# Two chunks at a time: smaller steps for norms and for the recurrence in a planned one-core kernel

## The chip, the core and the metric

The kernel runs on one core of one Trainium2 chip. TensorE (PE in the rows; PEld is its weight load) multiplies matrices, VectorE (DVE) and ScalarE (ACT) work on elements, GpSimd (POOL) does little here, and SyncE (SP) issues the loads. Each engine runs its own instructions in the order in which the program holds them, and waits where an operand or a buffer isn't ready. The metric is the time of one execution on the device, in microseconds; less is better.

## What is computed

Two transformer blocks over 256 tokens of width 1024, in float32. The first block is a self-attention with two kinds of heads, an attention to 256 memory rows, a gated feed-forward network with a short convolution, and a final norm. The second block has two layers over the latent tokens x and 256 context tokens ctx. Each layer modulates norms by a vector c and projects to three mixers: a neighbourhood attention, a two-way linear recurrence (RWKV-7) and a convolution. Layer 0 ends in a dense FFN for x and for ctx, layer 1 in a mixture of eight experts for x. Cut to its core:

```python
def first_block(x, mem, ...):
    u = rmsnorm(h, g_mix)
    h = h + norm(attention(u @ w_in)) @ w_out
    h = h + memory_cross_attention(rmsnorm(h, g_cross), rmsnorm(mem, g_mem))
    h = h + conv_ffn(rmsnorm(h, g_ffn))
    return rmsnorm(h, g_final)

def _rwkv7_scan(r, w, k, v, z, b):
    def step(S, inp):
        s_z = einsum('ghvk,ghk->ghv', S, z_t)
        S = S * w_t + s_z b_t^T + v_t k_t^T
        return S, einsum('ghvk,ghk->ghv', S, r_t)
    return lax.scan(step, zeros, (r, w, k, v, z, b))
```

The recurrence runs in both directions; each scans the context first and goes on into the latent tokens, and a norm per head (`_head_norm`) follows.

## The kernel before

Activations lie transposed, 8 chunks of 128 features by 256 tokens. A float32 product is made of three faster ones: each operand is split into a high and a low half (`whi`, `wlo` for weights; the pairs in `op`, `opM`, `fh` for activations), and `mm3` multiplies high by high, high by low and low by high. Weights come by 512 KB loads (`raw`), ScalarE rounds the high half (L306, L439) and VectorE subtracts for the low half (L307, L440). `products` (L467) emits 12 such matmuls a step, and every matmul has line L291.

The program is cut into stages by pools of buffers. B is the first block's attention beside the context's first projections and the modulation of layer 0. F+C0 is the first FFN (`first_ffn`, then `first_norm`) beside the context's recurrence (`rwkv(0, 1, ...)`) and mixing. A1 is the projections of the latent tokens (`latents`) beside the modulation of layer 1. C1 is the dense FFN of the context beside the latent recurrence (`rwkv(0, 0, ...)`) and mixing. A2 projects the context of layer 1 beside the dense FFN of x, C2 has the rest of that FFN beside a recurrence, C3 holds the last attention and recurrence, and M the experts.

What stands in what order is decided when the program is built. Each part is a Python generator that emits some instructions and then yields. `par` (L149) takes, of those that are ready, the one whose yielded cost over its weight is least, lets it emit up to its next yield, and so weaves the parts together. A yielded `Lat(wait, cost)` (L139) makes a generator unready until the others have spent `wait` in cost; it is a wait of the planner, which puts other instructions between, and no instruction of the chip:

```python
        cost = c.cost if isinstance(c, Lat) else c or 1.0
        e[0] += cost / e[3]
        spent += cost
        if isinstance(c, Lat):
            e[5] = spent + c
```

Work named `behind` fills in at its weight as long as a main part lives. The context's dense FFN (`dense_ffn(1, xc)`, called D1 below) is such work in F+C0, with weight 60, once the first FFN has stopped loading and the context's mixing is done; in A1 it is behind with 19, and in C1 it is a main part with 150 against 187.5. So whatever of it is emitted early is missing later. After that a scheduler moves single instructions within each engine's order.

A norm goes like this. `col_sums` puts sums of squares into a small bank (`sm<-bcst,ss`), `rsqrt` (L309 to L322) works on two columns on VectorE (`sc`), a matmul spreads the result over the partitions (`sm<-bcst,sc`), and `make_op` (L375) multiplies each of 8 chunks (L380) and splits it on ScalarE and VectorE (L382 to L386) for the next product. `norm_op` (L389) made all 8 chunks in one step, `first_norm` (L753) likewise. In the recurrence `rwkv` (L977) makes the unit keys `kk`, `rwkv_maps` (L1012) the decays and gates, and `rwkv_unit` (L1140) works a chunk of 128 features (i = 0, then 1, in each direction dr) through doubling steps of small matmuls (`c<-t,t`, `c<-t,zt`, `c<-cst,t`) each of which waits for the copy or the product of the step before (L301, L1260). `rwkv_scan` (L1043) carries the state (`S`, `Sb`) and ends in the norm per head.

Of the kernel before, what the change touches and what calls it, by code (L numbers as in the profile page):

```python
# [14 lines left out]
ALU = mybir.AluOpType  # L15
# [4 lines left out]
P = 128  # L20
T = 256
# [216 lines left out]
class K:  # L238
# [136 lines left out]
    def make_op(self, op, x, rb, A, B=None):  # L375

        nc = self.nc
        for c, (h, l) in enumerate(op):
            y = self.t("t1", [P, T])
            nc.vector.scalar_tensor_tensor(out=y, in0=x[:, c, :], scalar=A(c), in1=rb, op0=ALU.mult, op1=ALU.mult)  # L380
            if B is None:
                nc.scalar.activation(h, y, AF.Copy)  # L382
                nc.vector.tensor_tensor(out=l, in0=y, in1=h.bitcast(F32), op=ALU.subtract)
            else:
                nc.scalar.activation(h, y, AF.Identity, bias=B(c))  # L385
                nc.vector.scalar_tensor_tensor(out=l, in0=y, scalar=B(c), in1=h.bitcast(F32), op0=ALU.add,  # L386
                                               op1=ALU.subtract)

    def norm_op(self, x, A, B=None, tag="op"):  # L389
# [4 lines left out]
        self.make_op(op, x, rb, A, B)  # L394
        yield Lat(1.5)
# [303 lines left out]
    def first_attn(self, x, op):  # L699
# [35 lines left out]
        yop = self.new_op()  # L735
        for g in range(2):
            rb = yield from self.rstd(self.norm_sum(ys[g], C=4), 512, 1e-6)
            self.make_op(yop[4 * g:4 * g + 4], ys[g], rb, lambda c: self.v("g_out", 4 * g + c))
# [14 lines left out]
    def first_norm(self, x):  # L753
# [6 lines left out]
        yield 1.0  # L760
# [216 lines left out]
    def rwkv(self, l, s, u, S0, need_out, st):  # L977
# [10 lines left out]
        ps = self.head_sums(sq, "c0")  # L988
        nv = self.t("sc", [P, 16])[:, :8]
        nc.vector.tensor_scalar(out=nv, in0=ps[:, 0:8], scalar1=1.0, scalar2=1e-12, op0=ALU.mult, op1=ALU.add)  # L990
        kb = self.head_bc(self.rsqrt(nv, 8), "c0")
        kk = self.t("kk", [P, 2, T])
        for i in range(2):
            nc.vector.scalar_tensor_tensor(out=kk[:, i, :], in0=k_[:, i, :], scalar=self.v(f"k_k{l}", i),
                                           in1=kb[:, i, :], op0=ALU.mult, op1=ALU.mult)
# [8 lines left out]
        yield 2.0  # L1004
# [7 lines left out]
    def rwkv_maps(self, l, dr, u, kk, vt, need_out, st):  # L1012
# [7 lines left out]
        nc.gpsimd.memset(th[64:65, :], 1.0)  # L1020
        pp = self.ps2(tag)
# [16 lines left out]
        yield 1.7  # L1038
# [4 lines left out]
    def rwkv_scan(self, l, s, dr, u, S0, need_out, st):  # L1043
# [84 lines left out]
        rb = self.head_bc(self.rsqrt(nv, 8), tag)  # L1128
# [11 lines left out]
    def rwkv_unit(self, dr, i, sw, r, kk, kd, b, vt, tag, need_out, st):  # L1140
# [36 lines left out]
        ZB, ZK = self.t("zt", [P, 2, 2, P]), self.t("zt", [P, 2, 2, P])  # L1177
        px = self.ps2(tag).rearrange("p h (c e s) -> p h c e s", c=4, e=2)
# [476 lines left out]
    def program(self):  # L1655
# [66 lines left out]
        run(par((then(self.first_ffn(x), self.first_norm(x)), 173),  # L1722
# [126 lines left out]
```

## Time and profile before

| | us |
|---|---|
| median of 3 runs (lowest to highest) | 2905.23 (2900.95 to 2911.19) |
| the profiled execution | 2904.22 |
| its span in the trace | 2902.0 |
| PE busy | 2721.5 |
| DVE busy | 2130.2 |
| ACT busy | 1703.9 |

The profiled execution had a mean granted clock of 0.959 of 2.4 GHz. Rows of the trace name a line of the kernel, the engine, the operation and out<-in by the program's names without numbers; a bracket gives the engine's idle time just before and what ended it. `acc` is the bank of the FFNs, `accA` that of projections, `c` (c0, c1) that of the recurrence's two directions, `sm` the small one and `md` that of the modulation.

### The profile page before, as it was taken

Reading aid. Unit: us, or ns where it says so; the run is one execution under the profiler, and the core shown is the slowest. Engines: PE = TensorE matmul, PEld = TensorE weight load, DVE = VectorE, ACT = ScalarE, POOL = GpSimd, SP = SyncE. Lnnn points to the kernel's source line nnn. Section 1 sums busy time; section 2 is a strip of 40 time slices with the busy share of each in tenths; the row PEclk is TensorE's granted clock in tenths of the full one; section 3 lists DMA queues with packets and bytes.
Section 4 is the critical chain, followed back from the end, with each engine's and each line's share of the span. In section 5 each row is a group of like instructions: output and inputs, shape, how many; then the busy total and the mean of one; then the engine's idle time right before and its main releaser. Section 6 shows DMA issues by size and latency. Waiting matters only on the chain.

```text
span 2902.0 us, 55553 instructions
## 1 busy us (share of the span) xinstructions
PE 2721.5 (94%) x22026; PEld 2340.4 (81%) x22026; DVE 2130.2 (73%) x3912; ACT 1703.9 (59%) x2709; POOL 79.8 (3%) x229
## 2 busy tenths in 40 slices
PE   7899989999799899999998878799999999999998
PEld 5788888999787688999997866688888878887886
DVE  4458657777668466777566864689888889989897
ACT  4455555554454355455444553478777777777775
POOL 0000000100000000000000010000000000000000
PEclk9899998999899999999999987799999999999998
DMA  7666432345466723444443221479899999999994
GB/s 269 230 196 196 154 101 89 125 125 153 147 215 223 236 85 100 146 147 152 140 139 107 92 59 29 201 282 364 342 347 359 350 350 354 358 338 356 365 353 168
DMA packets 144022, 619.81 MB, mean 214 GB/s; under 512 B 31044, under 2 KB 38536, under 8 KB 100744
## 3 DMA queue, kind: packets, MB, share of 16 engines
q1 hardware_dynamic: 143752, 616.17, 61.0%
q8 instruction: 175, 2.87, 0.4%
q14 instruction: 95, 0.78, 0.1%
HBM read 615.04 MB, written 1.07 MB: 212 GB/s over the span
## 4 chain that ended last, share of the span: by engine, by line
PE 75%; DVE 8%; ACT 4%; issue 2%; DMA 2%; POOL 0%; SPq 0%; ACTq 0%; POOLq 0%; DVEq 0%
PE acc L291 42%; PE py L291 10%; PE accA L291 8%; PE sm L291 6%; PE c L291 6%; DVE wlo L307 1%; DVE wlo L440 1%; PE md L291 1%; PE sm L1571 1%; ACT whi L306 1%; PE accA L505 0%; DMA raw<-mod_w 0%; ACT whi L439 0%; DVE x L939 0%; DVE t L380 0%
## 5 line engine op out<-in xcount | busy, mean ns | idle before, releaser
L440 DVE TENSOR_TENSOR wlo<-raw,whi 128x1024 fp32r<-128x1024 f32 x666 | 779.4, 1220 | 79.8 <-ACT whi L439 73.0
L306 ACT ACTIVATE whi<-raw 128x512 fp32r<-128x512 f32 x764 | 474.3, 629 | 502.1 <-PE acc L291 259.7
L307 DVE TENSOR_TENSOR wlo<-raw,whi 128x512 fp32r<-128x512 f32 x764 | 521.3, 689 | 330.2 <-ACT whi L306 316.8
L439 ACT ACTIVATE whi<-raw 128x1024 fp32r<-128x1024 f32 x666 | 676.7, 1058 | 105.6 <-PE py L291 60.8
L291 PE MATMUL acc<-whi,op 128*128 128x512 f32 (+1 forms) x2048 | 620.8, 379 | 0.0
L291 PE MATMUL acc<-op,whi 128*128 128x256 f32 x2880 | 561.4, 294 | 8.7 <-ACT op L385 3.6
L291 PEld LDWEIGHTS acc<-op,whi 128*128 128x128 f32 x2880 | 460.1, 196 | 36.3 <-issue 13.8
L291 PEld LDWEIGHTS acc<-whi,op 128*128 128x128 f32 x2048 | 378.6, 189 | 71.5 <-issue 3.0
L291 PE MATMUL acc<-op,wlo 128*128 128x256 f32 x1440 | 414.7, 288 | 10.3 <-DVE wlo L307 10.3
L291 PE MATMUL acc<-wlo,op 128*128 128x512 f32 (+1 forms) x1024 | 393.0, 384 | 2.5 <-DVE wlo L440 1.4
L291 PEld LDWEIGHTS acc<-op,wlo 128*128 128x128 f32 x1440 | 281.5, 196 | 13.1 <-DVE wlo L307 12.7
L291 PE MATMUL py<-whi,ht 128*128 128x512 f32 x896 | 291.2, 396 | 0.5 <-ACT ht L306 0.5
L291 PE MATMUL accA<-opM,whi 128*128 128x256 f32 x1408 | 272.0, 292 | 7.7 <-ACT opM L306 3.5
L291 PEld LDWEIGHTS accA<-opM,whi 128*128 128x128 f32 x1408 | 225.0, 196 | 23.7 <-issue 7.7
L291 PEld LDWEIGHTS acc<-wlo,op 128*128 128x128 f32 x1024 | 193.2, 189 | 53.6 <-DVE wlo L440 17.6
L291 PE MATMUL acc<-fh,whi 128*128 128x256 f32 x1056 | 206.1, 293 | 3.0 <-ACT fh L306 1.9
L291 PE MATMUL accA<-opM,wlo 128*128 128x256 f32 x704 | 202.4, 288 | 1.5 <-DVE wlo L307 1.3
L291 PEld LDWEIGHTS py<-whi,ht 128*128 128x128 f32 x896 | 168.7, 188 | 39.3 <-ACT ht L306 0.9
L291 PE MATMUL py<-wlo,ht 128*128 128x512 f32 x448 | 180.6, 403 | 0.3
L291 PEld LDWEIGHTS acc<-fh,whi 128*128 128x128 f32 x1056 | 165.4, 192 | 18.4 <-issue 9.6
L291 PE MATMUL acc<-fh,wlo 128*128 128x256 f32 x528 | 150.4, 285 | 1.9 <-DVE wlo L307 1.9
L291 PEld LDWEIGHTS accA<-opM,wlo 128*128 128x128 f32 x704 | 137.3, 195 | 4.5 <-issue 2.2
(338 smaller groups left out, 3337.2 us busy)
## 6 DMA issues: line engine op xcount, KB each, us to landing
raw<-moe_up SPq DMA_DIRECT2D x112, 1024.0 KB, 7.0
raw<-moe_gate SPq DMA_DIRECT2D x111, 1024.0 KB, 6.8
raw<-moe_down SPq DMA_DIRECT2D x110, 1024.0 KB, 6.8
raw<-w_in SPq DMA_DIRECT2D x120, 512.0 KB, 3.7
raw<-mod_w SPq DMA_DIRECT2D x96, 512.0 KB, 4.5
raw<-ffn_gate SPq DMA_DIRECT2D x44, 512.0 KB, 3.6
raw<-ffn_up SPq DMA_DIRECT2D x44, 512.0 KB, 3.6
raw<-ffn_down SPq DMA_DIRECT2D x40, 512.0 KB, 3.7
```

Source lines behind the costliest of these rows:

```text
L291: return self.nc.tensor.matmul(out, lhsT, rhs, start=start, stop=stop, **k)
L306: self.nc.scalar.activation(hi, src, AF.Copy)
L307: self.nc.vector.tensor_tensor(out=lo, in0=src, in1=hi.bitcast(F32), op=ALU.subtract)
L439: self.nc.scalar.activation(hi, raw[:, k:k + g, :], AF.Copy)
L440: eng.tensor_tensor(out=lo, in0=raw[:, k:k + g, :], in1=hi.bitcast(F32), op=ALU.subtract)
L1571: nc.tensor.transpose(pt[:, c * P:(c + 1) * P], h[:, c * P:(c + 1) * P], self.ident)
```

## The change

Nothing is computed otherwise. `make_op` and `first_norm` now yield after every second chunk with a planner's wait of 1.4 and a cost of 0.2 (which `norm_op` and `first_attn` hand on), so that other parts' instructions stand between the pairs; the waits behind the whole norm go. In `rwkv` the transposes of v come first, and waits stand before the sums, before the spreading of the reciprocal root, and at the end. The maps, the unit and the scan's norm get declared waits. In F+C0 the weight of the first FFN falls from 173 to 155, so that the context's part beside it gets a larger share. All engines hold as many instructions as before, but for one more load of an activation table on ScalarE.

```diff
@@ make_op, norm_op, first_attn @@
                 nc.vector.scalar_tensor_tensor(out=l, in0=y, scalar=B(c), in1=h.bitcast(F32), op0=ALU.add,
                                                op1=ALU.subtract)
+            if c % 2:
+                yield Lat(1.4, 0.2)
...
         op = self.new_op(tag)
-        self.make_op(op, x, rb, A, B)
-        yield Lat(1.5)
+        yield from self.make_op(op, x, rb, A, B)
         return op
...
-            self.make_op(yop[4 * g:4 * g + 4], ys[g], rb, lambda c: self.v("g_out", 4 * g + c))
+            yield from self.make_op(yop[4 * g:4 * g + 4], ys[g], rb, lambda c: self.v("g_out", 4 * g + c))
@@ first_norm @@
             if c % 2:
                 self.add_squares(x, c // 2)
-        yield 1.0
+                yield Lat(1.4, 0.2)
@@ rwkv @@
-        ps = self.head_sums(sq, "c0")
...
-        kb = self.head_bc(self.rsqrt(nv, 8), "c0")
-        kk = self.t("kk", [P, 2, T])
...
         self.copy(vt.rearrange("p a b -> p (a b)"), pv)
-        yield 2.0
+        yield Lat(1.0, 0.6)
+        ps = self.head_sums(sq, "c0")
...
+        rn = self.rsqrt(nv, 8)
+        yield Lat(3.2, 0.3)
+        kb = self.head_bc(rn, "c0")
+        kk = self.t("kk", [P, 2, T])
...
+        yield Lat(1.0, 1.0)
@@ rwkv_maps @@
         nc.gpsimd.memset(th[64:65, :], 1.0)
+        yield Lat(0.7, 0.1)
...
         st["kd"][dr] = kd
-        yield 1.7
+        yield Lat(0.9, 1.6)
@@ rwkv_scan @@
-        rb = self.head_bc(self.rsqrt(nv, 8), tag)
+        rn = self.rsqrt(nv, 8)
+        yield Lat(3.0, 0.2)
+        rb = self.head_bc(rn, tag)
@@ rwkv_unit @@
         ZB, ZK = self.t("zt", [P, 2, 2, P]), self.t("zt", [P, 2, 2, P])
+        yield Lat(1.2, 0.2)
@@ program, F+C0 @@
-        run(par((then(self.first_ffn(x), self.first_norm(x)), 173),
+        run(par((then(self.first_ffn(x), self.first_norm(x)), 155),
```

What that does to the order is seen at three places. The first is PE at the start of A1. Before, 48 of D1's matmuls (`acc_9159<-op_9063` and its kin; op_9063 and op_9064 are the context's normed operand) stand behind `first_norm`'s spreading, and then come the modulation (`md`), the sums and the spreading of A1's norm, and its first products (`accA`):

```order
L291 MATMUL acc_9159<-op_9064,whi_9210 128x256
L291 MATMUL acc_9159<-op_9063,wlo_9211 128x256
L291 MATMUL md_9140<-raw_9141,cs_193 32x512 x2
L291 MATMUL md_9140<-raw_9142,cs_193 32x512 x2
L291 MATMUL md_9140<-raw_9226,cs_193 32x512 x2
L291 MATMUL md_9140<-raw_9227,cs_193 32x512 x2
L291 MATMUL sm_9190<-bcst_70,ss_9102 128x1 x4
L291 MATMUL sm_9234<-bcst_70,sc_9198 128x128 x2
L291 MATMUL acc_9295<-op_9063,whi_9273 128x256
L291 MATMUL acc_9295<-op_9064,whi_9273 128x256
L291 MATMUL accA_9318<-opM_9237,whi_9310 128x256
L291 MATMUL accA_9318<-opM_9238,whi_9310 128x256
```

Now 612 matmuls of D1 stand behind `first_norm`'s spreading, and more of them between the modulation, the sums (sm_10115) and the spreading (sm_10161):

```order
L291 MATMUL acc_10001<-op_9063,wlo_10017 128x256
L291 MATMUL md_10069<-raw_10070,cs_193 32x512 x2
L291 MATMUL md_10069<-raw_10071,cs_193 32x512 x2
L291 MATMUL acc_10001<-op_9063,whi_10032 128x256
...
L291 MATMUL acc_10102<-op_9063,wlo_10081 128x256
L291 MATMUL sm_10115<-bcst_70,ss_9078 128x1 x4
L291 MATMUL acc_10102<-op_9063,whi_10098 128x256
...
L291 MATMUL md_10069<-raw_10154,cs_193 32x512 x2
L291 MATMUL sm_10161<-bcst_70,sc_10123 128x128 x2
L291 MATMUL acc_10102<-op_9063,whi_10137 128x256
```

So some 560 matmuls of D1 moved from behind A1's norm to ahead of it and into it; A1 itself holds some 650 of D1 in either order.

The second place is PE in the latter half of C1, where the units i = 1 of both directions take their doubling steps (`c_...`, one name a direction and step). Before, 12 matmuls of D1 (`acc_13334`) stand between one direction's step and the other's:

```order
L291 MATMUL c_2379_13424<-t_2373_13385,zt_13025 64x64 x8
L291 MATMUL c_2379_13424<-cst_72,t_2373_13385 64x64 x8
L291 MATMUL c_2382_13445<-t_2375_13404,t_2376_13406 64x64 x8
L291 MATMUL acc_13334<-op_9063,whi_13408 128x256
L291 MATMUL acc_13334<-op_9064,whi_13408 128x256
L291 MATMUL acc_13334<-op_9063,wlo_13409 128x256
...
L291 MATMUL c_2387_13477<-t_2380_13441,t_2381_13443 64x64 x8
L291 MATMUL c_2389_13488<-t_2383_13454,zt_12975 64x64 x8
L291 MATMUL c_2389_13488<-cst_72,t_2383_13454 64x64 x8
L291 MATMUL acc_13513<-fh_13112,whi_13458 128x256
```

Now the same steps stand with nothing between:

```order
L291 MATMUL c_2523_14284<-t_2518_14259,t_2519_14261 64x64 x8
L291 MATMUL c_2525_14295<-t_2521_14280,t_2522_14282 64x64 x8
L291 MATMUL c_2527_14306<-t_2524_14293,zt_13969 64x64 x8
L291 MATMUL c_2527_14306<-cst_72,t_2524_14293 64x64 x8
L291 MATMUL c_2530_14327<-t_2526_14304,zt_14000 64x64 x8
L291 MATMUL c_2530_14327<-cst_72,t_2526_14304 64x64 x8
L291 MATMUL c_2533_14348<-t_2528_14323,t_2529_14325 64x64 x8
L291 MATMUL c_2535_14359<-t_2531_14344,t_2532_14346 64x64 x8
L291 MATMUL c_2537_14370<-t_2534_14357,zt_13969 64x64 x8
L291 MATMUL c_2537_14370<-cst_72,t_2534_14357 64x64 x8
```

D1's last matmul now stands at the start of the units i = 1. Before, 385 of D1's matmuls stood between there and the end of the norm per head, 48 among the mixing's products, and 216 behind them; of the 385 seven are left.

The third place is DVE at the start of F+C0, where the first FFN's operand (`op`, L380 and L383) and the recurrence's maps and first unit (`kd`, `d`, L1033 to L1170 before, L1038 and on now) are made. Before, the unit keys `kk` were followed by the maps and the unit:

```order
L994 SCALAR_TENSOR_TENSOR kk_4735<-u_82,vec_68,c_879_4726 128x256 x2
L1033 TENSOR_SCALAR kd_4754<-d_886_4753,vec_68,lv_148_724 128x256 x2
L1035 TENSOR_TENSOR kd_4754<-kd_4754,u_82 128x512
L1036 TENSOR_TENSOR d_886_4753<-d_886_4753,kk_4735 128x512
L1033 TENSOR_SCALAR kd_4772<-d_891_4771,vec_68,lv_148_724 128x256
L1164 TENSOR_TENSOR t_905_4819<-u_81,ptp_4806 128x4x64
...
L1170 TENSOR_TENSOR t_906_4822<-d_886_4753,t_901_4808 128x2x128
L380 SCALAR_TENSOR_TENSOR t_914_4848<-x_66,vec_68,sm_4843 128x256
...
L383 TENSOR_TENSOR op_4847<-t_914_4848,op_4846 128x256
L383 TENSOR_TENSOR op_4847<-t_915_4852,op_4846 128x256
```

Now the operand's chunks come straight after `kk`:

```order
L1006 SCALAR_TENSOR_TENSOR kk_4762<-u_82,vec_68,c_885_4753 128x256 x2
L380 SCALAR_TENSOR_TENSOR t_890_4770<-x_66,vec_68,sm_4765 128x256
L380 SCALAR_TENSOR_TENSOR t_891_4774<-x_66,vec_68,sm_4765 128x256
L380 SCALAR_TENSOR_TENSOR t_900_4801<-x_66,vec_68,sm_4765 128x256
L383 TENSOR_TENSOR op_4769<-t_890_4770,op_4768 128x256
L383 TENSOR_TENSOR op_4769<-t_891_4774,op_4768 128x256
...
L383 TENSOR_TENSOR op_4769<-t_906_4824,op_4768 128x256
L1038 TENSOR_SCALAR kd_4792<-d_898_4791,vec_68,lv_144_708 128x256
L383 TENSOR_TENSOR op_4769<-t_907_4828,op_4768 128x256
L1038 TENSOR_SCALAR kd_4792<-d_898_4791,vec_68,lv_144_708 128x256
L1040 TENSOR_TENSOR kd_4792<-kd_4792,u_82 128x512
```

The first FFN's chunks passed twelve instructions of the maps and the unit.

## Rows read from the trace of the kernel before

**Rows 1.** Page, part 1: busy time and share of each engine, instructions
```profile
PE 2721.5 (94%) x22026; PEld 2340.4 (81%) x22026; DVE 2130.2 (73%) x3912; ACT 1703.9 (59%) x2709; POOL 79.8 (3%) x229
```

**Rows 2.** Page, part 4: the chain that ended last, by engine
```profile
PE 75%; DVE 8%; ACT 4%; issue 2%; DMA 2%; POOL 0%; SPq 0%; ACTq 0%; POOLq 0%; DVEq 0%
```

**Rows 3.** Windows: stretch, length, busy (instructions) by engine, granted clock, DMA share, GB/s
```profile
758.80:778.10 19.30, 7.85 (x44) 5.67 (x45) 13.98 (x37) 8.23 (x17) 2.18 (x2) 0.67 0.42 134
765.50:779.00 13.50, 5.87 (x24) 5.28 (x25) 11.05 (x29) 5.71 (x12) 2.18 (x2) 0.50 0.32 92
424.20:454.70 30.50, 22.80 (x92) 17.55 (x93) 17.32 (x62) 14.68 (x24) 3.74 (x17) 0.50 0.11 35
278.00:298.00 20.00, 15.11 (x81) 13.45 (x80) 16.80 (x53) 7.98 (x17) 0.15 (x2) 0.74 0.48 154
85.00:104.00 19.00, 11.69 (x48) 6.41 (x47) 10.85 (x34) 8.89 (x22) 0.00 (x0) 0.64 0.77 259
1081.00:1177.00 96.00, 89.86 (x1319) 81.26 (x1316) 66.53 (x172) 46.53 (x90) 9.80 (x26) 0.97 0.32 98
1109.10:1129.20 20.10, 20.10 (x480) 18.38 (x483) 13.39 (x29) 8.75 (x18) 0.00 (x0) 1.00 0.27 82
1542.10:1558.50 16.40, 11.31 (x299) 9.51 (x290) 7.96 (x27) 7.56 (x16) 1.16 (x6) 1.00 0.01 2
1751.90:1768.90 17.00, 15.92 (x208) 10.99 (x210) 8.35 (x32) 7.02 (x21) 1.08 (x1) 0.50 0.01 2
1850.00:2880.00 1030.00, 1016.60 (x4618) 821.34 (x4618) 900.91 (x920) 775.18 (x886) 0.00 (x0) 0.99 0.90 339
```

**Rows 4.** Windows, PE's instructions on tile acc alone, in C1's second half
```profile
1081.00:1177.00 96.00, 55.12 (x385) 48.24 (x385) 5.56 (x11) 1.75 (x3) 0.97 0.32 98
```

**Rows 5.** Timeline of PE, A1's start: start, length, instruction, [idle before <-releaser]
```profile
763.48 1.05 PE L291 MATMUL sm<-bcst,ss 128*128 128x1 f32 x8 [2.85 <-DVE ss L333]
...
766.96 1.22 PE L291 MATMUL sm<-bcst,sc 128*128 128x128 f32 x4 [2.42 <-DVE sc L321]
...
771.14 0.79 PE L291 MATMUL accA<-opM,whi 128*128 128x256 f32 x2 [2.53 <-ACT whi L306]
...
775.58 0.58 PE L291 MATMUL acc<-op,wlo 128*128 128x256 f32 x1 [3.65 <-DVE wlo L307]
```

**Rows 6.** Timeline of PE, C0's start
```profile
448.29 1.23 PE L291 MATMUL c<-cst,d 128*128 128x128 f32 x4 [1.75 <-ACT d L1032]
...
450.87 2.08 PE L291 MATMUL c<-t,t 64*128 64x128 f32 x16 [1.35 <-DVE t L1170]
...
452.88 0.79 PE L291 MATMUL acc<-op,whi 128*128 128x256 f32 x2
```

**Rows 7.** Timeline of PE, doubling steps in the tails of C2 and C3
```profile
1542.17 0.41 PE L291 MATMUL c<-t,t 64*64 64x64 f32 x16
...
1546.21 0.46 PE L291 MATMUL c<-t,t 64*64 64x64 f32 x16 [0.19 <-ACT t L301]
...
1747.97 0.46 PE L291 MATMUL c<-t,t 64*64 64x64 f32 x16
...
1750.83 0.46 PE L291 MATMUL c<-t,t 64*64 64x64 f32 x16 [2.39 <-ACT t L301]
```

**Rows 8.** Timeline of PE, six single waits
```profile
91.17 2.37 PE L291 MATMUL md<-raw,cs 128*32 128x512 f32 x6 [3.61 <-DMA raw<-mod_w]
...
331.52 0.38 PE L291 MATMUL acc<-op,wlo 128*128 128x256 f32 x1 [3.49 <-DVE wlo L307]
...
1032.37 1.16 PE L291 MATMUL c<-t,t 64*128 64x128 f32 x16 [1.87 <-DVE t L1170]
...
1563.77 1.22 PE L291 MATMUL sm<-bcst,sc 128*128 128x128 f32 x4 [4.34 <-DVE sc L321]
...
1621.89 1.45 PE L291 MATMUL c<-t,t 64*128 64x128 f32 x12 [2.50 <-DVE t L1170]
...
1813.40 0.91 PE L291 MATMUL sm<-bcst,sc 128*64 128x128 f32 x6 [3.58 <-DVE sc L321]
```

More of the change, by code (lines that the diff above doesn't have):

```diff
@@ L987, in rwkv @@
             nc.scalar.activation(sq[:, i, :], k_[:, i, :], AF.Square, scale=self.v(f"k_k{l}", i))
-        ps = self.head_sums(sq, "c0")
-        nv = self.t("sc", [P, 16])[:, :8]
-        nc.vector.tensor_scalar(out=nv, in0=ps[:, 0:8], scalar1=1.0, scalar2=1e-12, op0=ALU.mult, op1=ALU.add)
-        kb = self.head_bc(self.rsqrt(nv, 8), "c0")
-        kk = self.t("kk", [P, 2, T])
-        for i in range(2):
-            nc.vector.scalar_tensor_tensor(out=kk[:, i, :], in0=k_[:, i, :], scalar=self.v(f"k_k{l}", i),
-                                           in1=kb[:, i, :], op0=ALU.mult, op1=ALU.mult)
         vt = self.t("vt", [P, 2, T])
@@ L1003, in rwkv @@
         self.copy(vt.rearrange("p a b -> p (a b)"), pv)
-        yield 2.0
+        yield Lat(1.0, 0.6)
+        ps = self.head_sums(sq, "c0")
+        nv = self.t("sc", [P, 16])[:, :8]
+        nc.vector.tensor_scalar(out=nv, in0=ps[:, 0:8], scalar1=1.0, scalar2=1e-12, op0=ALU.mult, op1=ALU.add)
+        rn = self.rsqrt(nv, 8)
+        yield Lat(3.2, 0.3)
+        kb = self.head_bc(rn, "c0")
+        kk = self.t("kk", [P, 2, T])
+        for i in range(2):
+            nc.vector.scalar_tensor_tensor(out=kk[:, i, :], in0=k_[:, i, :], scalar=self.v(f"k_k{l}", i),
+                                           in1=kb[:, i, :], op0=ALU.mult, op1=ALU.mult)
+        yield Lat(1.0, 1.0)
         yield from par(*[(self.rwkv_maps(l, dr, u, kk, vt, need_out, st), 45) for dr in range(2)],
```

## The prediction

> **What bounds the kernel now.** The first view is the busy time by engine: TensorE works 2721.5 us of a span of 2902.0, 94% [rows 1], and three quarters of the chain that ended last are its matmuls [rows 2]. The change removes no matmul, so at most the 180 us in which TensorE stands still, and what its lower clock costs, can be won. The second view is the table of stretches [rows 3]. In the last 1030 us, the experts, TensorE is busy 1016.6 us at a granted clock of 0.99: nothing to win, and the change doesn't touch that stage. What can be won lies before 1850 us, in a handful of places where a norm or the start of a recurrence leaves TensorE without work, and each is paid twice: by the idle time, and by the clock, which stands at 0.50 (1.2 instead of 2.4 GHz) in and after most of them. The third view, the order of time on TensorE, says who ends those waits: mostly the short norm operations on VectorE, or the low half of a weight (L307) that stands behind norm chunks on VectorE [rows 5, 6, 8].
>
> The sum below is made against the profiled execution, 2904.2 us, which is 1.0 us under the median of 2905.2.
>
> **Part 1, the start of A1 (a gain).** From 758.8 to 778.1 us TensorE has 7.85 us of work in 19.3 us [rows 3]. Four waits, 2.85, 2.42, 2.53 and 3.65 us, make 11.45 us [rows 5]; from 765.5 to 779.0 the clock is at 0.50, and 5.87 us of matmuls ran there that would take half, 2.9 us less [rows 3]. That is 14.4 us in all. The new order puts 564 more of D1's matmuls ahead of A1's norm and some between its steps. They need only the context's operand, which is there, and weights whose loads are queued. So the norm's steps on VectorE run under them. What can remain: D1's own splits share VectorE with the norm's chunks, as the wait of 3.65 us for L307 shows. I take 12, between 9 and 14. The wait of the final norm of block one just before stays; no free work can pass it in the new order.
>
> **Part 2, the start of F+C0 (a gain).** From 424.2 to 454.7 us TensorE is busy 22.8 of 30.5 us, all of it at 0.50 [rows 3]. The first FFN begins only at 452.88 us [rows 6], since its operand stands behind twelve operations of the recurrence's maps and unit on VectorE. Now it comes ahead of them, some 12 us earlier. Then the waits of 1.75 and 1.35 us [rows 6] are filled, 3.1 us, and the clock can rise earlier: at full speed the last 12 us would lose up to half. What is queued behind the chunks is the recurrence, which runs beside the FFN and ends before it. I take 6.5, with 3 (the waits alone) and 12 as ends.
>
> **Part 3, norms of the first block (a gain).** From 278 to 298 us 4.9 us are idle and the clock is 0.74, which costs 5 us more [rows 3]; the cross attention's norm leaves a wait of 3.49 us for a low half behind chunks [rows 8]. Pairs of chunks let the split in between. Of the 13 us I take 7.5, for both places together, since other streams' steps are short there; the ends are 0 and 13.
>
> **Part 4, the recurrences elsewhere (a gain).** The declared waits aim at waits such as 1.87 us at the start of C1, 2.50 us in C3 and 3.58 us at its last norm per head [rows 8]. They make 7.95 us, and there are smaller ones like them. In C3 there is attention to put between. I take 10 with the clock's part, from 0 to 15. Gains so far: 12 + 6.5 + 7.5 + 10 = 36 us.
>
> **Part 5, C1's latter half loses its cover (a loss).** What D1 fills at A1's start it doesn't fill in C1. Its matmuls cost the same wherever they stand, so this is no loss by itself; the loss is what they covered. From 1081 to 1177 us TensorE is busy 89.86 of 96 us [rows 3], 55.12 us of it by 385 of D1's matmuls, 0.143 us each [rows 4]. Without 378 of them 54.1 us leave, and 35.8 us of the recurrence's own work remain. How long does that take bare? The doubling steps from 1109.1 to 1129.2 us, four pairs, are all busy with 96 of D1's between [rows 3]: 20.1 less 13.7 leaves 6.4 us of own work. A bare pair took 4.04 us in C2's tail (1542.17 to 1546.21) and 2.86 us in C3's (1747.97 to 1750.83) [rows 7], so four take 11.4 to 16.2 us, and TensorE is busy 56% or 40%. The whole bare tail of C2 is busy 11.31 of 16.4 us, 69% [rows 3]. At 69% the 35.8 us take 52, at 56% 64. The half of C1 had 6.1 us idle already; so the exposed time is 52 - 35.8 - 6.1 = 10, or 22. With a lower clock it is more: from 1751.9 to 1768.9, at 0.50, 15.92 us of matmuls ran that would take about 8 at full speed [rows 3], and the upper end is some 34. I take 22, nearest the paired steps, which are the bulk of the half.
>
> Here a rule speaks against the change. The rows show both levels in bare recurrences: 1.00 in C2's tail with 69% busy, 0.50 in C3 [rows 3]. The Trainium skill, page "TensorE: Matmul & The Clock Gate", section "HAM oscillation — how this bites in real kernels", says that waits between bursts of matmuls let the array fall back to its lower rate, so that each burst starts slow. C3's stretch agrees with it, C2's tail doesn't; by the rule the loss would be the 34, and that is the second rival.
>
> **Part 6, smaller losses.** A2's norms were covered by D1's rest and now stand behind the mixing bare: the like wait at the end of C2 is 4.34 us [rows 8], and some of one is there already, so 2.5 (0 to 5). In the attention of the first block the modulation's matmuls go ahead of the projections, four more loads of 512 KB, and TensorE waits for such a load 3.61 us already [rows 8]; 2 MB at 259 GB/s [rows 3] are 8 us, partly beside softmax work, so 4 (0 to 8). The memory attention's first head has fewer projections beside it: 2 (0 to 4). The further load of a table on ScalarE costs nothing, hidden by an engine that is busy 59% [rows 1]; uncovered it would add a microsecond or two. Losses: 22 + 2.5 + 4 + 2 = 30.5 us.
>
> **The sum.** 2904.2 - 36 + 30.5 = 2898.7, and against the median 2899.7: I forecast **2900 us**, 0.2% less. A measurement of this kernel tells no change from one of about 0.3%, 8.7 us, so this is no change. Its own range is 2890 to 2912.
>
> **Rivals.** (a) Faster: the bare recurrence is cheap. If all of C1's half goes at the 69% of C2's tail and full clock, the loss there is 10 instead of 22, and with the smaller losses near 2 instead of 8.5 the time is 2899.7 - 12 - 6.5 = 2881. A half measure gives 2890. For it: C2's tail, at full clock throughout. Against it: the paired steps, 40 to 56%.
>
> (b) Slower: the bare half of C1 runs at the lower clock. The loss there is then 34 instead of 22, and A2's bare norms start slow too, 5 instead of 2.5; if the norms of the first block give nothing besides (0 instead of 7.5), the time is 2899.7 + 12 + 2.5 + 7.5 = 2922, and without that last 2914. It decides once the half takes longer than about 70 us bare, where it had 96 with 54 of D1's in it. For it: C3's stretch at 0.50. Against it: C2's tail.
>
> (c) The fills are worthless: the norms' waits move instead of vanishing, because VectorE has to make the same chunks and D1's low halves beside them. Then A1's start gives 9, C0's 3, the others nothing, 12 in all against the same 30.5: 2923 us. Against it: VectorE is idle 5 of the 19.3 us at A1's start [rows 3], and D1 gives it one split in 12 matmuls. That the planner's waits change nothing is excluded by the order itself, at A1 and C1.
>
> **How the numbers follow.** The forecast has 0.40, (a) 0.36, (b) 0.15, (c) 0.09. A fifth left out at the far ends of (a) and of (b) and (c) gives 2879 to 2921. Faster by over 0.3% is (a), 0.36, and a little of the forecast's lower end, 0.02: 0.38. Slower is (b) and (c), less what of them stays within 0.3%: 0.22. The rest, 0.40, is no change.
>
> **What would show it.** After the change the start of A1 should hold no wait over 1 us on TensorE between the final norm of block one and the first projection but the spreading's own, and a clock near 1.00; the first FFN should begin some 12 us sooner after the unit keys. C1's latter half should be about 64 us long, from the first product of the units i = 1 to the end of the norm per head, and idle for about 28 of them, with its clock telling (a) from (b). A half under 55 us would make me wrong towards faster, one over 75 us towards slower. The experts should take the same 1030 us. If the waits at A1's start are still there, with VectorE as their releaser, it is (c).

## The result: slower by 0.6%

The changed kernel took 2923.57 us, median of 12 runs (2915.34 to 2929.61), beside 2903.93 us of the kernel before (12 runs, 2895.37 to 2911.50). The ratio is 1.0063, with a 95% interval of 1.0050 to 1.0076. I had forecast 2900 us, no change, in a range of 2879 to 2921. The measured time lies above that range, and the kernel became slower, which I had held to be less likely than faster.

The page of the changed kernel answers [rows 1] and [rows 2]: the span went from 2902.0 to 2920.6 us, and TensorE is busy for 22.6 us more with the same number of instructions. The page alone doesn't say which of them took longer. The chain could be followed over a third of the span only, so its shares aren't compared.

```profile
PE 2744.1 (94%) x22026; PEld 2354.5 (81%) x22026; DVE 2130.8 (73%) x3912; ACT 1702.7 (58%) x2710; POOL 80.9 (3%) x229
...
PE 34%; DVE 2%; ACT 1%; issue 1%; DVEq 0%; ACTq 0%
```

The stretches that the prediction named look as follows in the changed kernel (stretch, length, busy time and instructions of PE, PEld, DVE, ACT and POOL, granted clock, DMA share, GB/s). They answer [rows 3].

```profile
430.60:461.30 30.70, 26.52 (x103) 22.07 (x104) 19.08 (x65) 15.17 (x26) 4.03 (x17) 0.50 0.11 35
444.00:461.30 17.30, 16.84 (x57) 13.16 (x56) 10.08 (x24) 10.97 (x19) 4.03 (x17) 0.50 0.00 1
764.80:838.00 73.20, 70.54 (x564) 69.53 (x564) 51.00 (x87) 36.98 (x60) 4.25 (x3) 0.97 0.55 169
838.00:872.00 34.00, 33.46 (x257) 27.84 (x256) 21.72 (x49) 15.47 (x30) 0.00 (x0) 1.00 0.75 255
1158.00:1225.00 67.00, 53.07 (x982) 44.03 (x982) 43.38 (x135) 25.38 (x57) 7.26 (x22) 0.83 0.07 21
1850.00:2900.00 1050.00, 1031.04 (x4747) 835.40 (x4747) 912.10 (x945) 785.80 (x904) 0.00 (x0) 0.99 0.90 336
```

The reader is to see three things. The run of D1 (764.8 to 838) and A1's norm behind it (838 to 872) are dense at nearly full clock, so the waits of [rows 5] are gone. C1's latter half (1158 to 1225) is bare: 67 us, 13.9 of them idle, at a clock of 0.83. And the start of F+C0 (430.6 to 461.3) is denser than before, 26.5 of 30.7 us against 22.8 of 30.5, but is still wholly at 0.50.

To see where the 18.6 us of the two profiled executions come from, I cut both at the same events on TensorE: the first matmul of F+C0's recurrence, the sums of block one's final norm, the first matmul of C1's recurrence, the first product of C1's mixing, and the first matmul of C2's and of C3's recurrence. The rows count the FFNs' matmuls (tile acc) in each stretch, first in the kernel before and then in the changed kernel:

```profile
427.10:745.20 318.10, 213.17 (x1584) 196.63 (x1584) 45.16 (x79) 12.21 (x22) 0.96 0.40 125
745.20:1003.00 257.80, 92.00 (x624) 82.16 (x624) 10.13 (x20) 2.98 (x5) 0.95 0.66 210
1003.00:1176.50 173.50, 98.20 (x696) 86.97 (x696) 10.45 (x21) 2.95 (x5) 0.98 0.32 99
1176.50:1316.30 139.80, 57.23 (x416) 55.27 (x416) 9.07 (x19) 1.71 (x3) 0.96 0.50 157
```

```profile
433.30:754.80 321.50, 219.67 (x1584) 201.58 (x1584) 45.17 (x79) 12.23 (x22) 0.95 0.39 124
754.80:1083.40 328.60, 172.49 (x1272) 160.63 (x1272) 20.54 (x41) 5.30 (x9) 0.98 0.65 208
1083.40:1224.80 141.40, 45.88 (x314) 39.88 (x312) 8.52 (x18) 1.18 (x2) 0.91 0.21 64
1224.80:1334.70 109.90, 21.17 (x152) 19.85 (x152) 0.68 (x1) 1.18 (x2) 0.95 0.46 147
```

In each fence the rows are F+C0, A1 from the final norm on, C1 up to the mixing, and mixing with A2. The last three hold 1736 of these matmuls in either kernel, but 624, 696 and 416 became 1272, 312 and 152 (two of the row's 314 began before the stretch). So these three stretches are compared as one: 571.1 us before, 579.9 after, 8.8 us lost. F+C0 lost 3.4 us, the program up to F+C0 6.2 us, and all behind C2's start 0.2 us (18.6 less the others).

### The profile page after: what moved, and what is told of

The parts are those of the page before. It is cut to its first block, busy times and chain, and to the rows that moved or that the text cites. A ratio compares the mean times of both kernels' runs of the same rounds, so it can differ in the third digit from the quotient of the medians.

```text
span 2920.6 us, 55563 instructions
## 1 busy us (share of the span) xinstructions
PE 2744.1 (94%) x22026; PEld 2354.5 (81%) x22026; DVE 2130.8 (73%) x3912; ACT 1702.7 (58%) x2710; POOL 80.9 (3%) x229
## 5 line engine op out<-in xcount | busy, mean ns | idle before, releaser
L291 PEld LDWEIGHTS accA<-opM,whi 128*128 128x128 f32 x1408 | 225.8, 196 | 24.1 <-issue 6.9
```

The costliest lines, as they stand in the source:

```text
L291: return self.nc.tensor.matmul(out, lhsT, rhs, start=start, stop=stop, **k)
```

## The experiments

Every kernel ran in 5 rounds beside the kernel before on the same chip; ratios are to those runs, with 95% intervals. The lengths of stretches come from one profiled execution of each kernel, cut as above; such an execution lay up to 12 us from its kernel's median, so only differences that come back in several kernels are used.

### Each edit alone

The first four kernels are the kernel before with one group of edits each. The diffs are the hunks of the change: `first_norm` for e1, `make_op`, `norm_op` and `first_attn` for e2, `rwkv`, `rwkv_maps`, `rwkv_scan` and `rwkv_unit` for e3, and the number 155 for e4.

> The kernel before, with the one edit that the final norm of block one yields after each pair of chunks. In the order of TensorE D1's matmuls move ahead of A1's norm, and 620 small matmuls of C1's latter half stand bare (before: 164). Theory 1, lost cover: A1's start gains 6 us, C1's half loses 13, the time is 2904 + 7 = 2911. Rival, the bare half costs nothing and the loss is elsewhere: 2904 - 6 = 2898.

> The kernel before, with the one edit that the operands of norms are made two chunks at a time. Theory 1: the modulation goes ahead of the attention of block one (12 of its rows before the first products there, before: 8) and costs 5 us by waiting for loads, the norms of block one give back about as much as they lose: 2909. Rival: the pairs win the idle time of those norms, as predicted: 2904 + 4 - 7.5 = 2900.

> The kernel before, with the declared waits of the recurrence alone. Theory 1: the start of C0 gives nothing, since the clock stays at its lower level until as late as before, and C2 and C3 lose some 6 us: 2908. Rival, as predicted: the waits win 6.5 us at C0's start and 10 in the others: 2888.

> The kernel before, with the weight of the first FFN 155 instead of 173 and nothing else. Theory 1: the context's part ends somewhat earlier beside the FFN and nothing is uncovered: within 3 us of 2904. Rival: the larger share is what lets D1 start early and uncovers C1: 2910 or more.

| edit alone | median us | ratio | interval |
|---|---|---|---|
| e1, final norm in pairs | 2911.54 | 1.0008 | 0.9997 to 1.0019 |
| e2, operands in pairs | 2911.96 | 1.0012 | 0.9998 to 1.0026 |
| e3, recurrence's waits | 2888.20 | 0.9922 | 0.9905 to 0.9939 |
| e4, share 155 | 2910.56 | 1.0021 | 1.0004 to 1.0038 |

The recurrence's waits are a clear gain of 0.8%, as the prediction had it and against my theory after the result. The share alone is a small loss. The other two alone can't be told from no change, though e1's trace shows both sides of the exchange (its one profile was 10 us above its median): D1 had 1284 matmuls between the final norm and C1 instead of 624. The four logs of the ratios sum to -0.0037, 11 us faster; together the edits were 18 us slower. So the edits don't add up, and the question became which of them interact ("meet" in what follows).

### Each edit left out

Four kernels are the changed kernel with one group as before.

> The changed kernel, with the final norm of block one in one step as before. The four edits alone sum to some 11 us less than before, all together cost 18 more, so 29 us come from two of them meeting. Theory 2: it is the pairs of the final norm with the recurrence's waits. They leave C1's latter half bare (here 142 small matmuls stand bare, with all edits 662), and declared waits there have nothing to put between: 2895. Rivals, another pair: 2921.

> The changed kernel, with the operands of norms made in one step as before. Theory 2: the pair is not in it, so only what the operands cost alone goes, 3 us: 2920. Theory 3, the operand's pairs ahead of the maps at C0's start are what takes the recurrence's gain away: 2892.

> The changed kernel, without the declared waits of the recurrence. All theories of a meeting with the recurrence's waits: the other three edits sum to 12 us alone, so 2916. If the three meet with each other instead: 2925 or more, with 620 small matmuls bare in C1's half.

> The changed kernel, with the weight of the first FFN 173 as before. Theory 2: only the 6 us of the share alone go: 2917; 524 small matmuls stand bare in C1's half instead of 662, which may win a few us more. Theory 4, the share meets the recurrence's waits, so that the context's part runs ahead of its cover in F+C0: 2890.

| left out | median us | ratio | interval |
|---|---|---|---|
| u1, final norm's pairs | 2905.36 | 0.9988 | 0.9967 to 1.0009 |
| u2, operands' pairs | 2903.52 | 0.9988 | 0.9971 to 1.0005 |
| u3, recurrence's waits | 2921.09 | 1.0062 | 1.0038 to 1.0087 |
| u4, share 155 | 2904.59 | 0.9992 | 0.9979 to 1.0005 |

No single pair is to blame: three of the four groups, left out, give some 20 us back each. The theory of one meeting pair fell. And in the company of the others the recurrence's waits are worth nothing (u3 against all four), though alone they win 0.8%. u2 shows more: its D1 has 1320 matmuls between the final norm and C1 and only 264 in C1, more uneven than the changed kernel, and yet the 20 us are back.

### What carries the recurrence's gain, and what the cover is worth

x3 is the kernel before with one wait alone; x1 is the changed kernel with the weight of D1 behind A1 lowered, which keeps D1 for C1; x4 is the kernel before with the recurrence's waits and the final norm's pairs, and x2 is x4 with the same lower weight.

```diff
@@ x3: rwkv_scan, before @@
-        rb = self.head_bc(self.rsqrt(nv, 8), tag)
+        rn = self.rsqrt(nv, 8)
+        yield Lat(3.0, 0.2)
+        rb = self.head_bc(rn, tag)
@@ x1 and x2: program, A1 @@
-                behind=(ffn, 19)))
+                behind=(ffn, 4)))
```

> The changed kernel, with the context's FFN behind A1 at weight 4 instead of 19. So less of it is emitted in A1, and C1's latter half is covered again (176 small matmuls stand bare, with the change 662). Lost cover as a cause: C1 gets back some 13 us and A1 gives up some 5: 2915. Rival, the bare half isn't what costs: 2923 or more, as A1 loses fill.

> The kernel before, with the recurrence's waits, the final norm of block one in pairs, and the context's FFN behind A1 at weight 4, which keeps C1 covered (142 bare). If both gains add up where the cover is kept: 2888 for the waits, 10 less at A1's start: 2878. If A1 needs the fill that is taken from it: 2888 or more.

> The kernel before, with one declared wait alone, that before the spreading in the scan's norm per head (3.0). Theory: this one carries the recurrence's gain, since it lets the norms of both directions run beside each other: 5 us at C1's end, 9 after C3, 3 in F+C0: 2888 to 2890. Rival, the gain is spread over the maps, the unit and the keys: 2900.

> The kernel before, with the recurrence's waits and the final norm of block one in pairs, weight 19 in A1 as before, so that C1's half is bare (692). Compared with the run at weight 4 it shows what the cover is worth. Lost cover: 10 us won in A1 and 16 lost in C1 against the recurrence's waits alone, 2894. Rival, a bare half is worse under declared waits: 2904.

| kernel | median us | ratio | interval |
|---|---|---|---|
| x1, changed, D1 at 4 in A1 | 2922.00 | 1.0057 | 1.0038 to 1.0075 |
| x2, waits, final norm's pairs, D1 at 4 | 2890.39 | 0.9945 | 0.9927 to 0.9963 |
| x3, the scan's wait alone | 2893.72 | 0.9945 | 0.9926 to 0.9963 |
| x4, waits, final norm's pairs | 2898.37 | 0.9975 | 0.9955 to 0.9994 |

x3 shows that one wait has 0.55% of the 0.78%. The order of time on TensorE at C1's norm per head, of the kernel before and then of x3, shows one place where it acts. Before, the two directions' reciprocal roots ran one behind the other, and the second one's spreading waited 3.62 us on VectorE. With the wait the planner emits both sums first, the chains run beside each other, D1 fills, and both spreadings follow without any idle time, in 1.97 us for 32 matmuls:

```profile
1168.94 1.09 PE L291 MATMUL sm<-bcst,sc 128*64 128x128 f32 x16 [0.58 <-DVE sc L321]
...
1174.64 1.97 PE L291 MATMUL sm<-bcst,sc 128*64 128x128 f32 x16 [3.62 <-DVE sc L321]
```

```profile
1165.50 1.97 PE L291 MATMUL sm<-bcst,sc 128*64 128x128 f32 x32
```

This place is 2 to 3 us of the 16 (C1 took 171.1 us in x3 and 173.5 before). The stages behind C2's start were 5.1 us shorter and F+C0 2.7; the rest isn't located.

x1 shows that giving C1 its cover back by starving A1 wins nothing that can be measured. Its rows on tile acc (A1, C1, mixing with A2) don't say why: C1 has its 696 matmuls again and A1 has 768, most of them in the run ahead of its norm, but A1, C1 and A2 together take 569.3 us, 10.6 less than in the changed kernel. This execution lay 12 us under its median, so a gain that its stretches show and its median lacks is left open. I had expected 2915, if the bare C1 were what costs; so that isn't shown by this run.

```profile
752.10:1032.00 279.90, 105.81 (x768) 97.55 (x768) 11.15 (x22) 3.51 (x6) 0.97 0.65 203
1032.00:1197.60 165.60, 98.92 (x696) 87.14 (x696) 13.56 (x28) 2.37 (x4) 1.00 0.33 104
1197.60:1321.40 123.80, 37.42 (x272) 35.84 (x272) 4.86 (x10) 1.75 (x3) 0.96 0.50 155
```

x4 against e3 has the final norm's pairs, and with them the run of D1, beside the recurrence's waits: 0.9975 against 0.9922, the intervals apart. There the run costs 0.5%, though alone (e1) it cost nothing that can be told. At the lower weight (x2) 0.3% of it seem to come back, but the intervals of x2 and x4 touch.

### The share, and pairs in one place

y1 is the kernel before with the recurrence's waits (e3) and pairs in A1's norm alone; y2 is e3 with the first FFN's weight at 200; y3 has both; y4 is the changed kernel at 200. (The flag in the cut goes through to `make_op` and turns its yields on.)

```diff
@@ y1 and y3: project @@
-        op = yield from self.mod_op(x, l, 0, s, "opM")
+        op = yield from self.mod_op(x, l, 0, s, "opM", l == 0 and s == 0)
@@ y4: program, F+C0 @@
-        run(par((then(self.first_ffn(x), self.first_norm(x)), 155),
+        run(par((then(self.first_ffn(x), self.first_norm(x)), 200),
```

> The kernel before, with the recurrence's waits and with pairs of chunks in A1's norm alone. If pairs pay where other work stands ready (the context's FFN and the modulation): A1 loses 75 us instead of 86 and the time is 2888 - 8 = 2880. If pairs cost wherever they stand: 2890 or more.

> The kernel before, with the recurrence's waits and the weight of the first FFN 200 instead of 173. If the share costs by its size (155 cost some 6 to 8 us in F+C0): 5 us less there, 2883. If 173 lies at the best or any change costs: 2888 or more.

> The kernel before, with the recurrence's waits, pairs in A1's norm alone and the weight 200. If both gains hold and add up: 2876. Else the better of the two others.

> The changed kernel, with the weight of the first FFN 200 instead of 155. C1's latter half is covered in this order (142 small matmuls bare instead of 662), since the context's mixing ends later and D1 starts later. If the share is what the four together fail by, since it both thins F+C0 and lets D1 run early: 2900 or less. If the meeting is between the other edits: 2915 or more.

| kernel | median us | ratio | interval |
|---|---|---|---|
| y1, waits, pairs in A1's norm | 2889.08 | 0.9938 | 0.9915 to 0.9960 |
| y2, waits, share 200 | 2887.85 | 0.9930 | 0.9907 to 0.9953 |
| y3, waits, both | 2880.40 | 0.9916 | 0.9889 to 0.9944 |
| y4, changed, share 200 | 2884.79 | 0.9923 | 0.9900 to 0.9946 |

y4 is the largest single step of all: one number, 155 to 200, takes some 40 us from the changed kernel. In this order the context's mixing ends only at 737.8 us, behind the sums of the final norm (734.9 us); the context's own norm, which D1 needs, comes after that, and the run of D1 ahead of A1's norm is gone. The rows on tile acc (F+C0, A1, C1, mixing with A2) have 624, 708 and 406 matmuls again. A1, C1 and A2 take 561.1 us together instead of 579.9, and F+C0 306.4 instead of 321.5:

```profile
428.50:734.90 306.40, 217.23 (x1584) 199.82 (x1584) 45.17 (x79) 12.27 (x22) 0.95 0.38 127
734.90:987.00 252.10, 88.42 (x624) 79.61 (x624) 10.06 (x20) 2.97 (x5) 0.98 0.69 218
987.00:1156.40 169.40, 100.85 (x708) 89.42 (x708) 10.45 (x21) 2.96 (x6) 0.99 0.31 102
1156.40:1296.00 139.60, 55.05 (x406) 52.92 (x404) 9.03 (x19) 1.75 (x3) 0.96 0.48 159
```

On top of the recurrence's waits neither the pairs in A1 (y1) nor the share (y2) wins anything that can be told, so both of those expected gains failed, although the profiles show them in their stages: A1 took 254.7 us in y1 and 263.8 in e3, and F+C0 302.1 in y2 and 311.5 in e3. y3 has the lowest median, but its interval and those of e3, y1, y2 and y4 overlap widely: the versions at 2880 to 2889 us can't be ranked by these runs.

### The run of D1 by itself

The last two kernels separate the share from the run of D1. The context's FFN may form its operand as in the changed kernel, but emit products only when the final norm is written; z1 keeps 155, z2 has 173.

```diff
@@ dense_ffn @@
         op = yield from self.mod_op(x, 0, 1, s, "op")
+        if s:
+            yield lambda: self.normed
@@ first_norm @@
                 yield Lat(1.4, 0.2)
+        self.normed = True
```

> The changed kernel at its share of 155, but the context's FFN may begin its products only when the final norm of block one is written. So its run of 612 matmuls ahead of A1's norm is gone (48 as before), C1's latter half is covered (142 small matmuls bare) and all else is as changed. If the run is the cause: 2923 less the 20 us of C1 and with a few back at A1's start, 2905, like the change without the final norm's pairs. If the share costs in F+C0 alone: 2918 or more.

> The same at the share of 173. If the share costs a further 8 us in F+C0: 2897, between the gated one at 155 and the 2885 at 200. If the run is all: the same as the gated one at 155.

| kernel | median us | ratio | interval |
|---|---|---|---|
| z1, changed, D1 held back | 2901.77 | 0.9993 | 0.9977 to 1.0009 |
| z2, the same at 173 | 2896.64 | 0.9972 | 0.9960 to 0.9984 |

z1 gives back 20 us (1.0063 to 0.9993, intervals far apart) by nothing but the gate that holds D1 back. Its rows (F+C0, A1, C1, mixing with A2) stand against those of the changed kernel above: the last three take 561.7 us instead of 579.9, 18 less, and F+C0 is as long as there.

```profile
428.80:752.20 323.40, 219.96 (x1584) 201.70 (x1584) 45.20 (x79) 12.22 (x22) 0.95 0.38 123
752.20:1001.70 249.50, 93.07 (x624) 81.87 (x624) 10.16 (x20) 2.95 (x5) 0.98 0.67 216
1001.70:1174.30 172.60, 102.63 (x720) 90.89 (x720) 10.44 (x21) 2.96 (x6) 0.98 0.31 99
1174.30:1313.90 139.60, 53.93 (x394) 51.85 (x392) 9.07 (x19) 1.74 (x3) 0.96 0.48 160
```

With all of TensorE's instructions counted, A1 and C1 of the changed kernel and then of z1 show where the 18 us are:

```profile
754.80:1083.40 328.60, 312.56 (x2348) 266.21 (x2349) 211.61 (x492) 159.16 (x313) 11.46 (x15) 0.98 0.65 208
1083.40:1224.80 141.40, 123.51 (x2047) 106.96 (x2045) 94.94 (x260) 66.22 (x130) 15.74 (x45) 0.91 0.21 64
```

```profile
752.20:1001.70 249.50, 233.25 (x1700) 186.56 (x1701) 159.30 (x406) 116.68 (x245) 12.59 (x15) 0.98 0.67 216
1001.70:1174.30 172.60, 166.12 (x2454) 150.12 (x2454) 119.40 (x304) 91.04 (x172) 14.58 (x45) 0.98 0.31 99
```

In A1 TensorE is idle for 16.0 and 16.2 us, so the run saved nothing there. In C1 it is idle for 17.9 us at a clock of 0.91 with the run, and for 6.5 us at 0.98 without.

The surprise is A1: without the run ahead of its norm it takes 249.5 us, 8.3 less than before the change with the same 624 matmuls. The waits on TensorE from 752 to 800 us in z1 (waiting, releaser: total, times, longest) are short:

```profile
PE sm L292 <- DVE ss L334: 3.5, 1, 3.5
PE acc L292 <- ACT op L386: 2.5, 2, 1.3
PE sm L292 <- DVE sc L322: 1.4, 1, 1.4
PE acc L292 <- DVE wlo L308: 1.3, 1, 1.3
PE accA L292 <- DVE wlo L308: 1.1, 1, 1.1
```

The first of these is the wait of the final norm itself. So the pairs of both norms, with D1 woven in at its own weight, do away with most of the waits of [rows 5]; the 612 matmuls ahead of them weren't needed for that. Pairs in A1's norm alone aren't enough: in y1 the last two of the four waits are short, but those before the sums and the spreading stand as before:

```profile
749.93 1.05 PE L291 MATMUL sm<-bcst,ss 128*128 128x1 f32 x8 [2.85 <-DVE ss L333]
753.40 1.22 PE L291 MATMUL sm<-bcst,sc 128*128 128x128 f32 x4 [2.42 <-DVE sc L321]
```

The run is a second way to fill the same waits: in e1 and u2, which have it and no pairs in A1's norm, only one of them is left (4.41 and 3.59 us, before the first low half of a weight). That may be how u2 can have the run and not its loss: there it has a use, and beside the pairs it has none. It isn't shown by itself.

z2 against z1 is the share in F+C0 alone: 0.2%, like e4 alone. The stretch of F+C0 says the same in every pair that differs by 155 or 173 only: 318.1 us before and 326.3 in e4, 314.6 in z2 and 323.4 in z1, 314.3 in u4 and 321.5 in the changed kernel, 307.1 in x4 and 317.2 in u2. That is 7 to 10 us in each, and y4's 306.4 at 200 goes on the same way. The run and the share also meet: the run costs 0.7% at 155 (the changed kernel against z1) and 0.2% at 173 (u4 against z2, whose intervals touch), where 406 matmuls are left for C1 instead of 312. Where the share's time goes was followed in one pair only. In e4 the scan's spreading at the end of the recurrence waits 3.48 us, and the clock of the 60 us around it is 0.91; at the answering place before, the clock was 1.00 (one row of the time order and two windows, e4's and then that of the kernel before):

```profile
655.83 1.97 PE L291 MATMUL sm<-bcst,sc 128*64 128x128 f32 x16 [3.48 <-DVE sc L321]
```

```profile
640.00:700.00 60.00, 55.56 (x444) 53.94 (x444) 42.31 (x93) 26.70 (x46) 0.00 (x0) 0.91 0.43 140
```

```profile
643.00:703.00 60.00, 57.49 (x493) 55.18 (x492) 43.76 (x100) 27.58 (x47) 0.00 (x0) 1.00 0.46 146
```

## Why the prediction was wrong

Of the 24.1 us by which the two profiles miss the forecast's sum, 9.9 lie in F+C0, 8.2 behind C2's start and 7.7 ahead of F+C0; A1 to A2 came out 1.7 better than forecast. So the steps that failed are the clock of part 2 and the share that had no term, part 4, and the losses of part 6 ahead of F+C0. And one premise of parts 1 and 5 failed without showing in their sum.

**Parts 1 and 5: the sum came out, the premise didn't hold.** Their terms, with A2's and C1's start (-12 + 22 + 2.5 - 2), came to +10.5 us for A1 to A2; the profiles gave +8.8. The bare half of C1 took 67 us, forecast 64, so it was between the forecast and rival (b), and under the 70 us from which (b) was to decide. But it idled only 13.9 us where I expected about 28: the rest of the lost time is in matmuls at the lower clock, 0.83 on average. One pair of bare steps took 2.66 us at full clock, even less than the 2.86 of [rows 7]:

```profile
1195.61 0.46 PE L291 MATMUL c<-t,t 64*64 64x64 f32 x16 [0.32 <-ACT t L301]
...
1198.27 0.46 PE L291 MATMUL c<-t,t 64*64 64x64 f32 x16 [0.18 <-ACT t L301]
...
1221.18 3.68 PE L291 MATMUL sm<-bcst,sc 128*64 128x128 f32 x32 [1.65 <-DVE sc L320]
```

The last row is C1's norm per head: 1.65 us of waiting where two waits made 4.2. By the rule of the Trainium skill ("TensorE: Matmul & The Clock Gate", section "HAM oscillation — how this bites in real kernels") bursts of matmuls that follow waits start slow, and I had drawn from it a half at the lower clock as the second rival. The row shows 0.83, so a part of the half was slow: the trace agrees in part.

What the two parts missed is that two edits fill the same waits. I gave the gain at A1's start to the 564 matmuls of D1; z1 has it without them, by the pairs of the norms. So in the changed kernel the run was a pure loss, 20 us, and not a trade; where it was a trade (e1), it came out even.

**Part 2, the start of F+C0: the order was right, the clock was not.** The first FFN began at 444.08 us, 8.8 us sooner in spite of a later start of the stage, and the waits were filled. But I let the clock rise with the work. It stayed at 0.50 up to 461.3 us, while TensorE was busy 16.84 of the last 17.3 us, so the FFN's first matmuls ran at the lower clock: 50 us into the stage 157 of them had run, and 154 before the change. The failed step is the sentence that the clock "can rise earlier".

The runs also show which edit did what here. The early start of the FFN comes with the recurrence's waits: 10.8 us into the stage in every kernel that has all of them, with or without the operands' pairs, and 25.8 us in every other. And in the kernels that have these waits and not the operands' pairs in this stage the clock did rise earlier, after 20.4 us (x4, y1, y3) or 27.3 us (e3, u2, x2, y2) at 0.50, against 30.7 before the change and in the changed kernel. With the operands' pairs fewer of the FFN's matmuls run at first: 48 in the changed kernel's first 30 us, 93 in y1's, of which the clock itself is a part (rows on tile acc):

```profile
433.30:463.30 30.00, 12.22 (x48) 10.27 (x48) 0.00 (x0) 0.00 (x0) 0.53 0.11 36
```

```profile
423.60:453.60 30.00, 14.77 (x93) 13.22 (x94) 1.91 (x4) 1.10 (x2) 0.71 0.20 70
```

In e3, F+C0 took 311.5 us, the 6.6 less than before that part 2 had forecast as 6.5.

**The share had no term at all.** Part 2 spoke of F+C0's start and not of the weight of 155, though it is one of the edits. It cost 7 to 10 us within F+C0 in four pairs of kernels. It isn't what lets D1 run: with the final norm's pairs D1 runs at 173 as well (1284 matmuls ahead of C1 in e1 and x4, 1178 in u4), and only at 200 it doesn't (y4). Forecast for F+C0 -6.5, measured +3.4 by the profiles: 9.9 us of the miss.

**Parts 3 and 6 ahead of F+C0.** The program up to F+C0 lost 6.2 us where -7.5 + 4 + 2 = -1.5 was forecast. In the changed kernel TensorE waits three times for the modulation's loads, and then 3.79 us for a softmax step on VectorE:

```profile
94.30 1.05 PE L291 MATMUL md<-raw,cs 128*32 128x512 f32 x4 [1.23 <-DMA raw<-mod_w]
96.95 4.83 PE L291 MATMUL md<-raw,cs 128*32 128x512 f32 x16 [1.60 <-DMA raw<-mod_w]
102.82 1.05 PE L291 MATMUL md<-raw,cs 128*32 128x512 f32 x4 [1.04 <-DMA raw<-mod_w]
107.66 0.88 PE L506 MATMUL sm<-bcst,t 128*128 128x128 f32 x3 [3.79 <-DVE t L573]
```

This softmax step stood at 98.03 us before, 9.6 us earlier, so the term of 4 us was too small. Its reason failed, too: the waits for loads make 3.9 us now and made 4.9 before. What came on top are 16 more of the modulation's matmuls, and 1.4 us more of waiting for the softmax step (3.79 us, and 2.40 before). The norms of block one did gain. From the sums of the norm behind the first attention to those of the next norm TensorE now runs 40 matmuls more in 1.4 us less, at full clock, since projections fill its waits (before, then changed):

```profile
273.00:319.40 46.40, 41.51 (x293) 37.15 (x292) 35.95 (x94) 21.79 (x43) 0.15 (x2) 0.89 0.49 158
```

```profile
278.10:323.10 45.00, 43.05 (x333) 37.10 (x330) 40.29 (x105) 25.18 (x50) 0.00 (x0) 1.00 0.63 209
```

But these projections are missing behind: from there to F+C0 it takes 110.2 us instead of 107.7, with 28 matmuls fewer. That was the term of 2 us for the memory attention, and it was too small as well. How much of the 6.2 us is chance isn't settled: over the nine kernels with all the operands' pairs F+C0 began at 428.7 us on average (421.9 to 433.3), over the eleven others at 425.5 (423.0 to 428.4). So some 3 us are likely the pairs'.

**Part 4, the other recurrences.** I took 10 us for single waits, and behind C2's start 8 of it; the profiles gave a loss of 0.2. The waits aimed at did go, the 2.50 us in C3 and the scan's last 3.58 us ([rows 8]), but in C3 another took their place. A product of the recurrence's gates stands behind the attention's softmax, 6.59 us where the like wait before was 1.89 (first the changed kernel, then the kernel before):

```profile
1750.67 1.65 PE L291 MATMUL sm<-t,g 128*128 128x256 f32 x3 [6.59 <-ACT t L903]
```

```profile
1726.48 1.13 PE L291 MATMUL sm<-t,g 128*128 128x256 f32 x4 [1.89 <-ACT t L902]
```

This comes with the recurrence's waits, and the other edits don't do it: the wait is 6.78 us in e3 and 6.75 in u2, and 1.8 to 1.9 in e1, u3 and x3. In e3, too, all behind C2's start is only some 2 us shorter than before. So the step that failed is that each wait counts by itself, and the 0.8% of e3 were not won where part 4 put them; by its profile the clearest part of them lies in F+C0. That e3 alone came out at the 2888 us which the prediction's terms give for it was in part luck.

**The rivals.** Two gave nearly the right time for a wrong reason. (b) had 2922 with a half of C1 over 70 us long and nothing from the first block's norms; the half took 67 and the norms gained. (c) had 2923: it wanted waits on VectorE at A1's start, and between 838 and 872 us the longest wait of the changed kernel is for a load:

```profile
859.17 1.05 PE L291 MATMUL md<-raw,cs 128*32 128x512 f32 x4 [0.42 <-DMA raw<-mod_w]
```

Fill that is spent at a place where another edit already does its work stood in no rival.

**What stays open.** With D1 held back and 173 (z2) the changed kernel has the recurrence's waits and pairs in all norms, and is at 0.9972; the waits alone are at 0.9922. The pairs alone cost 0.12% (e2). So some 0.4% still don't add up, and at 200 (y4, 0.9923) they do. A part lies at F+C0: at 173 it takes 307.1 to 311.5 us in the kernels with the waits and no operands' pairs there (e3, x2, x4, y1), and 314.3 and 314.6 with both (u4, z2), the low clock of part 2. No run isolates this, nor the rest. Open, too, is which of the later places pays for the run: C1 is bare and slower in the changed kernel, but x1 gave C1 its matmuls back and its median won nothing.

## What to carry to other kernels

Work that fills in behind others is finite: before a wait is declared anywhere, ask which ready work the planner will put there, how much of it that spends, where it will be missing, and whether another of your edits fills the same gap already. A wait pays where a long chain has a twin that can run beside it, as the two directions' norms here. And when several such edits are made at once, measure them one by one and each left out: here one of four won 0.8%, the four together lost 0.6%, and one number decided between the two.

## What the runs showed of the hardware

The granted clock doesn't follow dense work at once: it stood at 0.50 for 17.3 us in which TensorE was busy for 16.84 (444.0 to 461.3 us above). And the spread between executions of one kernel goes mostly with the clock. The 12 runs of the changed kernel go from 2915.3 us at a mean clock of 0.959 to 2929.6 us at 0.955; over all kernels' runs the time falls by 1.8 us for each thousandth of mean clock (correlation -0.86 within kernels). Of e3's gain of 20 us that would be 12: its mean clock was 0.9635 and that of the kernel before, run beside it, 0.9569. That the clock and not the idle time alone carries it is read from this correlation and not tested by itself.
